# A planned decoder step: sample probabilities spread by one transfer per head pair, second-norm squares summed on VectorE, and other planner figures

## The chip, the cores and the metric

The kernel runs on one core of a Trainium2 chip. The metric is device time in microseconds (us) of one execution, the median of several runs. The engines are called as the profile calls them: PE (TensorE, the matmuls; PEld its weight loads), DVE (VectorE), ACT (ScalarE), POOL (GpSimd), SP (SyncE, which issues all DMAs here). TensorE's clock has two levels, 1.2 and 2.4 GHz; the "granted clock" of a stretch is its share of the higher one.

## What is computed

One inference step of a hybrid decoder layer, for a prompt of 1024 tokens and 8 sample tokens, 1032 columns together, in float32 with d_model 1024:

```python
h = rmsnorm(x, norm1_g)
a, gate, q, k, v, cx, cb, cc, u = split(h @ w_in, 9)     # 256 columns each
ya = silu(layernorm(causal_conv31(a * sigmoid(gate))))
ob = dilated_attention(q, k, v)      # 4 heads of 64; windows (128,1) (512,4) (2048,16)
yc = cb * causal_conv3(cc * cx)
yd = multi_pool(u) @ pool_w * pool_scale
x = x + concat(ya, ob, yc, yd) @ w_out
g, u = split(rmsnorm(x, norm2_g) @ w_gu, 2)
x = x + (silu(g) * u) @ w_down
y = rmsnorm(x, final_g)
# for a sample token: softmax over 3 * 129 cached or own keys per head, then p @ v
```

The outputs are y and the new states: key and value caches, the convolutions' last rows and the pooling's last rows.

## The kernel before, in words

All activations are held transposed, features on the 128 partitions and tokens along the row. The 1032 columns are cut in three chunks of 384, 256 and 392 (c = 0, 1, 2); the last holds the 8 sample tokens. Weights and activations are split into a high and a low part (ACT copies the high part, DVE subtracts), so each product takes three matmuls; the gate, up and down products use a seven-product Strassen scheme on top.

**Stages in time.** Input projection, prompt attention, convolutions and pooling run to about 320 us; the output projection with the second norm from there to about 420; gate and up products to about 850; down products to about 1090; then the last norm.

**What sets the order.** The kernel is written as streams (generators that yield one operation at a time). `Sched.run` picks among them at build time with a cost model of its own: `ready` says when an operation's operands are there, `emit` adds its cost, and the earliest one, with some preference by priority, is emitted next. The result is a fixed order for each engine. On the chip every engine takes its instructions in that order and waits by semaphores.

**DMAs.** `dma` issues on SP's queue. Each transfer uses one of eight semaphores in turn, so that SP waits for the landing of the one eight issues before it. Tiles come from small pools: `rw0/rw1` for raw weights, `t0..t7` for work tiles, `ta0..ta6` for the sample attention, four PSUM banks `mm0, mm1, ac0, ac1` for products.

**The sample attention.** The softmaxed probabilities of 8 samples and 4 heads are a 32x384 tile `s32` (row 4n + head). They are written to DRAM (`psd`). For each sample n and head pair i, `weigh` loads 128x384 gathered values (`vg`), loads two rows of `psd` so that each fills 64 partitions, and DVE multiplies and sums along the row into `o8` (`tensor_tensor_reduce`, an ISA row in the order, line 1329). Sixteen such steps run beside the output projection. The prompt's mixer outputs pass through DRAM as well (`ccT`).

**The second norm.** For each m (8 row blocks of x) and c, `add_x2` adds the projection to x on DVE (`x2[m]`, tiles g7, g9, g10, g15, g14, g16, g11, g0), ACT squares it, and POOL (`ptt`, line 386) adds the squares over m into one tile. `stat2` sums it over partitions with a matmul (`mi`), DVE makes the reciprocal root (`rs_n`), and a matmul (`st`) spreads it. After chunk 2 the first gate products (`raw_pair`, plain float32 at line 398) stand around that sum. x2 is written to DRAM (`x2d`) and read back by `x2_back` in the down stage.

Of the kernel before, what the change touches and what calls it, by code (L numbers as in the profile page):

```python
# [15 lines left out]
MUL, ADD, SUB, MAX = ALU.mult, ALU.add, ALU.subtract, ALU.max  # L16
# [11 lines left out]
DBLK = [[0, 1], [2, 3], [4, 5], [6, 7], [8, 9], [10]]  # L28
# [18 lines left out]


class Op:
    __slots__ = ("eng", "cost", "reads", "writes", "fn", "dep", "size")  # L50

    def __init__(self, eng, cost, reads, writes, fn, size=0):
        self.eng, self.cost, self.fn, self.size = eng, cost, fn, size
        self.reads = [region(a) for a in reads]
        self.writes = [region(a) for a in writes]
        self.dep = None


PLACE = {}
# [15 lines left out]
class Sched:  # L75
# [9 lines left out]
    def __init__(self):  # L85
        self.clock = {"pe": 0.0, "act": 0.0, "dve": 0.0, "pool": 0.0, "sp": 0.0}
        self.hw = self.dma = 0.0
        self.acc = {}
        self.streams = []
        self.log = []  # L90
        self.now = 0.0

    def add(self, prio, name, it):
        self.streams.append([prio, name, it, None])

    def ready(self, op):
        if op.dep is not None:
            return op.dep
        t = 0.0
        eng = op.eng  # L100
        for regs, wr in ((op.reads, False), (op.writes, True)):
            for k, p0, p1, f0, f1 in regs:
                for q0, q1, g0, g1, end, w, e in self.acc.get(k, ()):
                    if (w or wr) and q0 < p1 and p0 < q1 and g0 < f1 and f0 < g1:
                        if e == eng:
                            lat = 0.0 if eng in ("pe", "act") else 0.13
                        else:
                            lat = 0.2 if "pe" in (e, eng) else 0.14
                        t = max(t, end + lat)
        return t  # L110

    def emit(self, st, op):
        s = max(self.clock[op.eng], self.ready(op))
        if op.size:
            self.clock[op.eng] = s + 0.06
            self.hw = max(self.hw, s) + 0.45
            self.dma = max(self.dma, self.hw + 0.65) + op.size / 358e3
            end = self.dma + 0.95
        else:
            cost = op.cost * (2 if op.eng == "pe" and s < self.WARM else 1)  # L120
            self.clock[op.eng] = end = s + cost
        eng = "dma" if op.size else op.eng
        for regs, w in ((op.reads, False), (op.writes, True)):
            for k, p0, p1, f0, f1 in regs:
                l = self.acc.setdefault(k, [])
                if w:
                    l[:] = [x for x in l if not (p0 <= x[0] and x[1] <= p1 and f0 <= x[2] and x[3] <= f1)]
                else:
                    l[:] = [x for x in l if x[5] or x[6] != eng or not (p0 <= x[0] and x[1] <= p1 and f0 <= x[2] and x[3] <= f1)]
                l.append((p0, p1, f0, f1, end, w, eng))  # L130
        r = op.fn()
        self.log.append((op.eng, s, end, st[1], getattr(getattr(r, "ins", None), "name", None)))
# [8 lines left out]
    def run(self):  # L141
        self.waits = {}
        while self.streams:
            moved = True
            while moved:
                moved = False
                for st in list(self.streams):
                    while st[3] is None or (not isinstance(st[3], Op) and st[3]()):
                        try:
                            st[3] = next(st[2])  # L150
                            moved = True
                        except StopIteration:
                            self.streams.remove(st)
                            moved = True
                            break
            if not self.streams:
                break
            best = {}
            for st in self.streams:
                if st[1] == "main":  # L160
                    w = str(self.blocked(st)) if not isinstance(st[3], Op) else "op"
                    if w != getattr(self, "lastw", None):
                        self.lastw, self.t0 = w, self.now
                    elif w != "op":
                        self.waits[round(self.t0, 1)] = (round(self.now - self.t0, 1), w)
                op = st[3]
                if not isinstance(op, Op):
                    continue
                t = max(self.clock[op.eng], self.ready(op))
                best.setdefault(op.eng, []).append((t, st[0], st))  # L170
            if not best:
                raise RuntimeError("stuck: " + ", ".join(f"{x[1]} {self.blocked(x)}" for x in self.streams))
            pick = None
            for eng, l in best.items():
                t0 = min(x[0] for x in l)
                c = min((x for x in l if x[0] <= t0 + self.win(x[1])), key=lambda x: (x[1], x[0]))
                if pick is None or c[0] < pick[0]:
                    pick = c
            st = pick[2]
            op, st[3] = st[3], None  # L180
            self.now = pick[0]
            self.emit(st, op)
# [98 lines left out]
def get(slots, **kw):  # L281
    if not slots.free:
        def cond():
            return bool(slots.free)
        cond.why = slots.tag
        while not slots.free:
            yield cond
    return slots.alloc(**kw)


def wait(cond):
    if not cond():
        yield cond
# [16 lines left out]
def emit(nc, I, O, pools):  # L310
    PLACE.clear()
    S = Sched()
# [14 lines left out]
    def has(*f):  # L327
        return lambda: all(x in flags for x in f)
# [18 lines left out]
    def nfree(a):  # L347
        n = 1
        for _, m in list(a.ap)[1:]:
            n *= m  # L350
        return n
# [33 lines left out]
    def ptt(out, a, b, op):  # L385
        return pool(lambda: GP.tensor_tensor(out, a, b, op), out, (a, b))  # L386
# [4 lines left out]
    def mcost(r):  # L391
        n = nfree(r)
        if r.dtype == F32R:
            return max(0.112, n / 2400 + 0.0133)
        return 2 * max(0.107, n / 1200 + 0.0025)

    def mm(out, l, r, start, stop):
# [2 lines left out]
    def mms(out, items):  # L400

        def go():
            for o, l, r, a, b in items:
                i = PE.matmul(o, l, r, start=a, stop=b, skip_group_check=True)  # L404
            return i
        return Op("pe", sum(mcost(r) for _, _, r, _, _ in items), [x for i in items for x in i[1:3]], (out,), go)

    def trs(out, items):
        def go():
            for o, a, d in items:  # L410
                i = PE.transpose(o, a, d)  # L411
            return i
        return Op("pe", 0.109 * len(items), [x for _, a, d in items for x in (a, d)], (out,), go)

    def dma(out, in_, eng="sp"):
        n = 4
        for _, m in out.ap:
            n *= m
        q = {"sp": nc.sync, "act": nc.scalar, "pool": nc.gpsimd}[eng]
        return Op(eng, 0.06, (in_,), (out,), lambda: q.dma_start(out, in_), size=n)  # L420

    def split(hi, lo, src):
        yield act(hi, src, AF.Copy)
# [219 lines left out]
    for b, js in enumerate(DBLK):  # L643
        for mp in range(4):
            n = len(js) * 512
# [624 lines left out]
    def sample():  # L1270
# [51 lines left out]
        def weigh(n, i):  # L1322
            v = yield from get(TA, shape=[128, 384])
            yield dma(v, I["vg"][n, i])
            b = yield from get(TA, shape=[128, 384])
            for hh in range(2):
                yield dma(b[64 * hh:64 * hh + 64, :], psd[4 * n + 2 * i + hh, :].partition_broadcast(64))
            m = o8[:, i, n:n + 1]
            yield dve(lambda: V.tensor_tensor_reduce(v, v, b, 1.0, 0.0, MUL, ADD, m), v, (v, b), extra=(m,))
            TA.rel(v, b)  # L1330
            todo[0] -= 1
# [43 lines left out]
    def add_x2(m, c, p, sq, fl):  # L1375
        q, n = cols(c), CN[c]
        yield tt(x2[m][:, q], p[:, 0:n], x2[m][:, q], ADD)
        MM.rel(p)
        t = yield from get(TT)
        yield act(t[:, 0:n], x2[m][:, q], AF.Square)  # L1380
        if (sq, c) not in ssq:
            ssq[sq, c] = t
        else:
            s = ssq[sq, c]
            yield ptt(s[:, 0:n], s[:, 0:n], t[:, 0:n], ADD)
            TT.rel(t)
        flags.add(fl + (m, c))

# [153 lines left out]

    def x2_back():
        for m in range(8):
            t = yield from get(G, shape=[128, T])
            yield dma(t, x2d[m])
            x2[m] = t
            flags.add(("x2", m))
# [185 lines left out]

    def calm():

        yield from wait(lambda: S.dma < S.now + 3.5)

    def hload():
        for b, js in enumerate(DBLK):  # L1740
# [416 lines left out]
```

## Time and profile before

| | us |
|---|---|
| median of 3 runs | 1115.37 (1114.7 to 1115.53) |
| profiled execution | 1119.55 |
| its span, first to last instruction | 1117.8 |
| PE busy | 1088.2 (97%) |
| DVE busy | 921.0 (82%) |
| ACT busy | 497.6 (45%) |
| POOL busy | 48.3 (4%) |

The rows that follow come from the profiled execution. Times in them are us from the start of its span. A view of windows gives the busy time of each engine in a stretch; the timeline merges equal instructions and gives, in brackets, the idle time of the engine just before and what ended it; the chain is followed back from the last instruction to what released each step. The DMA view counts packets and lists the transfers by what they write and read.

### The profile page before, as it was taken

To read this page: it belongs to the slowest core of one execution; us is meant where nothing else is said; L and a number is where in the kernel's file an instruction comes from. 1 tells how busy PE (TensorE), PEld (TensorE's weight loads), DVE (VectorE), ACT (ScalarE), POOL (GpSimd) and SP (SyncE) were. 2 spreads that over 40 slices of the span, in tenths; PEclk is the share of its full clock that TensorE was granted. 3 is DMA by queue.
4 is the path that set the end of the run, shared out by engine and by line. 5 is a ranking of instruction groups with operands and counts; after the bars stand their busy time and mean duration, and the time that the engine had idled before them with its cause. 6 is when DMAs were issued, how large, how long until landed. Compare 5 with 4: busy or idle time off the path is not lost.

```text
span 1117.8 us, 21986 instructions
## 1 busy us (share of the span) xinstructions
PE 1088.2 (97%) x8167; PEld 1054.9 (94%) x8167; DVE 921.0 (82%) x2281; ACT 497.6 (45%) x1125; POOL 48.3 (4%) x63
## 2 busy tenths in 40 slices
PE   8999999999998999999999999999999999999995
PEld 5799998999998998999999999999999999999995
DVE  5999999866655498978878777887886999999977
ACT  6564633645533244535444444443543433333332
POOL 0000000000002240000000000000000000000033
PEclk9999999999999998999999999999999999999997
DMA  8042224534388423557457566655638999693103
GB/s 298 1 162 90 102 83 137 198 122 158 117 273 278 153 88 118 178 192 265 170 199 256 172 210 224 209 187 174 204 120 270 388 363 325 229 322 124 38 21 133
DMA packets 104395, 205.39 MB, mean 184 GB/s; under 512 B 11552, under 2 KB 65104, under 8 KB 103760
## 3 DMA queue, kind: packets, MB, share of 16 engines
q1 hardware_dynamic: 104288, 203.99, 53.7%
q8 instruction: 64, 1.05, 0.4%
q14 instruction: 43, 0.35, 0.1%
HBM read 150.98 MB, written 86.87 MB: 213 GB/s over the span
## 4 chain that ended last, share of the span: by engine, by line
PE 70%; DVE 15%; DMA 6%; ACT 2%; issue 2%; SPq 1%; POOL 0%; DVEq 0%; ACTq 0%; POOLq 0%
PE mm L404 37%; PE ac L404 28%; DVE g L369 5%; DVE g L372 2%; DMA t<-kg 2%; PE st L404 2%; DMA ta<-psd 2%; DVE wo L372 1%; DVE t L372 1%; DVE ta L372 1%; DVE h L372 1%; PE st L411 1%; SPq L420 1%; PE mm L398 1%; DMA t<-ccT 1%
## 5 line engine op out<-in xcount | busy, mean ns | idle before, releaser
L404 PE MATMUL mm<-h,wo 128*128 128x256 f32 (+3 forms) x3012 | 475.7, 302 | 3.4 <-ACT wo L362 3.4
L404 PEld LDWEIGHTS mm<-h,wo 128*128 128x128 f32 x3012 | 431.3, 189 | 6.7 <-ACT wo L362 3.5
L404 PE MATMUL ac<-h,wo 128*128 128x256 f32 (+3 forms) x1830 | 273.3, 289 | 0.0
L404 PEld LDWEIGHTS ac<-h,wo 128*128 128x128 f32 x1830 | 248.6, 189 | 0.0
L404 PE MATMUL mm<-g,wo 128*128 128x260 f32 (+1 forms) x879 | 126.4, 282 | 0.0
L404 PEld LDWEIGHTS mm<-g,wo 128*128 128x128 f32 x879 | 114.0, 189 | 0.0
L362 ACT ACTIVATE g<-g 128x260 fp32r<-128x260 f32 (+2 forms) x203 | 75.2, 413 | 83.9 <-DVE g L372 82.2
L372 DVE TENSOR_TENSOR g<-mm,g 128x260 f32<-128x260 f32 (+3 forms) x203 | 85.7, 425 | 27.3 <-PE mm L404 25.2
L404 PE MATMUL ac<-g,wo 128*128 128x260 f32 (+1 forms) x735 | 107.2, 283 | 0.0
L372 DVE TENSOR_TENSOR wo<-rw,wo 128x512 fp32r<-128x512 f32 x140 | 96.2, 690 | 8.8 <-ACT wo L362 8.3
L362 ACT ACTIVATE wo<-rw 128x512 fp32r<-128x512 f32 x140 | 87.1, 625 | 31.1 <-PE mm L404 19.8
L404 PEld LDWEIGHTS ac<-g,wo 128*128 128x128 f32 x735 | 96.2, 189 | 0.0
L372 DVE TENSOR_TENSOR g<-g,g 128x260 f32<-128x260 f32 (+4 forms) x195 | 80.8, 435 | 14.1 <-ACT g L362 7.3
L362 ACT ACTIVATE wo<-t 128x512 fp32r<-128x512 f32 (+1 forms) x103 | 60.8, 590 | 64.0 <-DVE t L372 46.4
L386 POOL TENSOR_TENSOR t<-t,t 128x256 f32<-128x256 f32 (+3 forms) x44 | 43.7, 992 | 886.0 <-ACT t L362 719.3
L369 DVE SCALAR_TENSOR_TENSOR g<-g,parh,g 128x1024 f32<-128x1024 f32 (+2 forms) x90 | 81.6, 923 | 0.4
L372 DVE TENSOR_TENSOR g<-g 128x260 fp32r<-128x260 f32 (+3 forms) x201 | 79.5, 424 | 2.7 <-ACT g L362 2.4
L372 DVE TENSOR_TENSOR g<-ac,g 128x256 f32<-128x256 f32 (+3 forms) x139 | 59.4, 427 | 24.6 <-PE ac L404 20.9
L372 DVE TENSOR_TENSOR wo<-t,wo 128x512 fp32r<-128x512 f32 (+1 forms) x103 | 65.3, 634 | 11.3 <-ACT wo L362 8.8
L362 ACT ACTIVATE t<-g 128x256 f32<-128x256 f32 (+4 forms) x90 | 40.0, 455 | 65.2 <-DVE g L372 47.5
L372 DVE TENSOR_TENSOR g<-t,g 128x260 f32<-128x260 f32 (+4 forms) x151 | 62.3, 431 | 2.5 <-ACT g L362 1.9
L404 PE MATMUL mm<-ta,wo 128*128 128x256 f32 (+1 forms) x357 | 61.6, 281 | 0.4 <-DVE g L372 0.4
(169 smaller groups left out, 1199.4 us busy)
## 6 DMA issues: line engine op xcount, KB each, us to landing
hd<-g SPq DMA_DIRECT2D x74, 260.0 KB, 3.4
hd<-g SPq DMA_DIRECT2D x74, 256.0 KB, 4.2
out_k_old<-cache_k SPq DMA_DIRECT2D x16, 1023.5 KB, 6.1
out_v_old<-cache_v SPq DMA_DIRECT2D x16, 1023.5 KB, 6.8
h<-hd SPq DMA_DIRECT2D x49, 256.0 KB, 6.0
g<-w_gu SPq DMA_DIRECT2D x22, 512.0 KB, 4.2
rw<-w_gu SPq DMA_DIRECT2D x22, 512.0 KB, 4.5
h<-hd SPq DMA_DIRECT2D x40, 260.0 KB, 6.0
```

What stands on the lines that cost most here:

```text
L362: lambda: AE.activation(out, in_, func, **kw))
L369: return dve(lambda: V.scalar_tensor_tensor(out, a, s, b, op0, op1), out, (a, s, b), ptr=aps(s))
L372: return dve(lambda: V.tensor_tensor(out, a, b, op), out, (a, b))
L386: return pool(lambda: GP.tensor_tensor(out, a, b, op), out, (a, b))
L398: return Op("pe", mcost(r), (l, r), (out,), lambda: PE.matmul(out, l, r, start=start, stop=stop, skip_group_check=True))
L404: i = PE.matmul(o, l, r, start=a, stop=b, skip_group_check=True)
L411: i = PE.transpose(o, a, d)
L420: return Op(eng, 0.06, (in_,), (out,), lambda: q.dma_start(out, in_), size=n)
```

## The change

Two operations change. `weigh` spreads its two probability rows with one transfer instead of two. The seven additions of squares of chunk 2 go from POOL to DVE; those of the other chunks stay. The rest changes the planner's figures, and so the order: dearer and later DMAs, 0.4 us of spare time for PE work outside the main stream behind producers other than DMAs, 0.8 us behind DMAs for everything that isn't a DMA, a small surcharge for a wide matmul behind a narrow one, a longer DMA backlog that loads of hidden tiles may meet (`calm`), and `x2_back` waits for block 0's last hidden tile from its fifth tile on. Line numbers after the change are 4 to 6 higher.

```diff
@@ class Sched @@
-    def ready(self, op):
-        if op.dep is not None:
-            return op.dep
+    SPARE, LATE = 0.4, 0.8
+
+    def ready(self, op, spare=0.0, late=0.0):
...
-                            lat = 0.2 if "pe" in (e, eng) else 0.14
+                            lat = (0.2 if "pe" in (e, eng) else 0.14) + (late if e == "dma" else spare)
...
-            self.hw = max(self.hw, s) + 0.45
-            self.dma = max(self.dma, self.hw + 0.65) + op.size / 358e3
-            end = self.dma + 0.95
+            self.hw = max(self.hw, s) + 0.5
+            self.dma = max(self.dma, self.hw + 0.7) + op.size / (300e3 if op.thin else 356e3)
+            end = self.dma + 1.2
...
+            if op.eng == "pe":
+                cost += 0.085 if self.short and not op.thin else 0.0
+                self.short = op.thin
...
-                t = max(self.clock[op.eng], self.ready(op))
+                side = op.eng == "pe" and st[1] != "main"
+                t = max(self.clock[op.eng], self.ready(op, self.SPARE if side else 0.0, 0.0 if op.size else self.LATE))
@@ mcost, trs, dma @@
-            return max(0.112, n / 2400 + 0.0133)
+            return max(0.112, n / 2400 + (0.0133 if n < 300 else 0.0155))
...
-        return Op("pe", 0.109 * len(items), [x for _, a, d in items for x in (a, d)], (out,), go)
+        return Op("pe", 0.112 * len(items), [x for _, a, d in items for x in (a, d)], (out,), go, thin=True)
...
-        return Op(eng, 0.06, (in_,), (out,), lambda: q.dma_start(out, in_), size=n)
+        return Op(eng, 0.06, (in_,), (out,), lambda: q.dma_start(out, in_), size=n, thin=nfree(out) < 512)
@@ weigh @@
-            for hh in range(2):
-                yield dma(b[64 * hh:64 * hh + 64, :], psd[4 * n + 2 * i + hh, :].partition_broadcast(64))
+            yield dma(b[:, :], psd[4 * n + 2 * i:4 * n + 2 * i + 2, :].unsqueeze(1).to_broadcast([2, 64, 384]))
@@ add_x2 @@
-            yield ptt(s[:, 0:n], s[:, 0:n], t[:, 0:n], ADD)
+            yield (ptt if c < 2 else tt)(s[:, 0:n], s[:, 0:n], t[:, 0:n], ADD)
@@ x2_back @@
         for m in range(8):
+            if m > 3:
+                yield from wait(has(("hl", 0, 1, 4, len(DBLK[0]) - 1)))
             t = yield from get(G, shape=[128, T])
@@ calm @@
-        yield from wait(lambda: S.dma < S.now + 3.5)
+        yield from wait(lambda: S.dma < S.now + 5)
```

**SP's queue at the first spreads** (ta tiles are the sample attention's; ccT loads feed the output projection), before:

```order
L420 DMA psd_76<-s32_3151 32x384
L420 DMA ta2_24_3277<-vg 128x384
L420 DMA ta4_25_3278<-vg 128x384
L420 DMA ta6_27_3282<-psd_76 64x384 x2
L420 DMA ta5_26_3280<-psd_76 64x384
L420 DMA t3_197_3300<-ccT_74 128x256
L420 DMA t6_198_3301<-ccT_74 128x256
L420 DMA t0_199_3302<-ccT_74 128x256
```
and after:

```order
L425 DMA psd_76<-s32_3147 32x384
L425 DMA ta2_24_3329<-vg 128x384
L425 DMA ta4_25_3330<-vg 128x384
L425 DMA ta6_26_3332<-psd_76 128x1x384
L425 DMA ta5_27_3334<-psd_76 128x1x384
L425 DMA rw0_19_3379<-w_out 128x1024
L425 DMA ta0_28_3391<-vg 128x384
L425 DMA ta3_29_3393<-psd_76 128x1x384
L425 DMA ta2_30_3399<-vg 128x384
```
The spreads are single 128x1x384 transfers, the ccT loads of chunk 1 have gone ahead of the psd write, and w_out tiles stand between the spreads.

**DVE behind the last products** (ISA rows; g14 is x2 of m=4, h20 the sample chunk's operand, rs_n20 the second norm's chain for chunk 0), before:

```order
L1329 ISA ta3_55_3748,o8_3276<-ta3_55_3748,ta1_56_3750 128x384
L1329 ISA o8_3276 128x1
L372 TENSOR_TENSOR g15_39_3479<-ac1_20_3790,g15_39_3479 128x256
L372 TENSOR_TENSOR pself_3269<-smp_72,pself_3269 128x8
L372 TENSOR_TENSOR g13_27_1163<-pself_3269,o8_3276 128x8
L372 TENSOR_TENSOR pself_3269<-smp_72,pself_3269 128x8
L372 TENSOR_TENSOR g6_35_2706<-pself_3269,o8_3276 128x8
L372 TENSOR_TENSOR h20_3_3483<-g13_27_1163,h20_3_3483 128x392
```
and after:

```order
L1333 ISA ta1_55_3878,o8_3328<-ta1_55_3878,ta0_56_3880 128x384
L1333 ISA o8_3328 128x1
L376 TENSOR_TENSOR pself_3320<-smp_72,pself_3320 128x8
L376 TENSOR_TENSOR g13_27_1207<-pself_3320,o8_3328 128x8
L376 TENSOR_TENSOR pself_3320<-smp_72,pself_3320 128x8
L376 TENSOR_TENSOR g6_35_2752<-pself_3320,o8_3328 128x8
L376 TENSOR_TENSOR h20_3_3463<-g13_27_1207,h20_3_3463 128x392
L376 TENSOR_TENSOR g14_40_3797<-ac1_22_3953,g14_40_3797 128x256
L376 TENSOR_TENSOR h20_3_3463<-g6_35_2752,h20_3_3463 128x392
L381 TENSOR_SCALAR rs_n20_4028<-mi0_14_4024 128x3
L381 TENSOR_SCALAR rs_n20_4028<-rs_n20_4028 128x3
L380 TENSOR_SCALAR rs_n20_4028<-rs_n20_4028 128x3
```
In the new order the chain of chunk 0 stands right behind the last product; before, w_out splits and six x2 adds stood between.

**PE at the broadcast of that chain** (st1_123; ac0_23 is the bank of m=7, chunk 1), after:

```order
L408 MATMUL mm0_59_4037<-h10_2_3243,wo8_49_3713 128x256 x6
L408 MATMUL ac0_23_4082<-h10_2_3243,wo1_52_3822 128x256 x3
L408 MATMUL st1_123_4078<-t6_228_4068,ones_68 128x128 x3
L408 MATMUL ac0_23_4082<-h10_2_3243,wo1_52_3822 128x256 x3
L408 MATMUL ac0_23_4082<-h10_2_3243,wo0_51_3757 128x256 x6
L408 MATMUL ac0_23_4082<-h10_2_3243,wo1_52_3822 128x256 x6
```
and before, where the broadcast st2_123 stands behind all products of its bank:

```order
L404 MATMUL ac0_23_4049<-h10_2_3299,wo9_50_3767 128x256 x6
L404 MATMUL ac0_23_4049<-h10_2_3299,wo8_49_3746 128x256 x6
L404 MATMUL st2_123_4095<-t4_228_4084,ones_68 128x128 x3
L404 MATMUL ac1_24_4093<-h10_2_3299,wo1_52_3814 128x256 x6
L404 MATMUL ac1_24_4093<-h10_2_3299,wo0_51_3791 128x256 x6
L404 MATMUL ac1_24_4093<-h10_2_3299,wo1_52_3814 128x256 x6
```
It has moved 21 matmuls ahead.

## Rows read from the trace of the kernel before

**Rows 1.** The page, busy time of each engine and its share of the span.

```profile
PE 1088.2 (97%) x8167; PEld 1054.9 (94%) x8167; DVE 921.0 (82%) x2281; ACT 497.6 (45%) x1125; POOL 48.3 (4%) x63
```

**Rows 2.** Timeline at two waits of PE: start, us, what, idle time before it.

```profile
347.49 1.81 PE L404 MATMUL mm<-h,wo 128*128 128x384 f32 x7 [3.37 <-ACT wo L362]
...
419.97 1.80 PE L404 MATMUL mi<-ones,t 128*128 128x1 f32 x8 [2.87 <-POOL t L386]
```

**Rows 3.** Windows: PE, PEld, DVE, ACT, POOL busy; PE's granted clock, DMA share, GB/s.

```profile
299.00:360.00 61.00, 57.63 (x362) 57.23 (x362) 31.90 (x86) 21.63 (x49) 5.26 (x6) 0.97 0.80 255
...
417.00:422.00 5.00, 2.13 (x10) 2.03 (x10) 4.93 (x13) 3.45 (x7) 1.10 (x1) 0.81 0.74 255
422.00:428.00 6.00, 6.00 (x18) 4.79 (x18) 4.92 (x19) 1.54 (x3) 0.00 (x0) 0.59 0.00 0
```

**Rows 4.** Instructions that read psd: issue ns min/median/max, first and last start.

```profile
L420 SPq DMA_DIRECT2D ta<-psd x32: 444/487/1904, 302.0 to 351.0; - x32
```

**Rows 5.** Chain that ends last, 299 to 362, one piece: start, us, what.

```profile
318.31 7.79 DMA ta<-psd
```

**Rows 6.** Timeline of DVE around the last products of the sample attention.

```profile
356.75 0.54 DVE L1329 CUSTOM_DVE_ANT_0 ta<-ta,ta 128x384 f32<-128x384 f32 x1
...
371.51 0.16 DVE L377 TENSOR_SCALAR rs_n<-mi 128x3 f32<-128x3 f32 x1 [2.25 <-PE mi L404]
```

**Rows 7.** Timeline of PE at the broadcast of the second norm's first chunk.

```profile
372.12 2.98 PE L404 MATMUL ac<-h,wo 128*128 128x256 f32 x24
375.19 0.94 PE L404 MATMUL st<-t,ones 128*128 128x128 f32 x6
```

**Rows 8.** The page: GB/s in 40 slices, packet counts, the main DMA queue.

```profile
GB/s 298 1 162 90 102 83 137 198 122 158 117 273 278 153 88 118 178 192 265 170 199 256 172 210 224 209 187 174 204 120 270 388 363 325 229 322 124 38 21 133
DMA packets 104395, 205.39 MB, mean 184 GB/s; under 512 B 11552, under 2 KB 65104, under 8 KB 103760
...
q1 hardware_dynamic: 104288, 203.99, 53.7%
```

**Rows 9.** DMA issues: transfers, KB of each, median us from issue to landing where known.

```profile
rw<-w_out SPq DMA_DIRECT2D x12, 512.0 KB, 5.6
...
g<-xR SPq DMA_DIRECT2D x8, 516.0 KB, 5.7
...
ta<-vg SPq DMA_DIRECT2D x16, 192.0 KB, 3.7
...
x2d<-g SPq DMA_DIRECT2D x8, 320.0 KB, 2.8
...
t<-ccT SPq DMA_DIRECT2D x6, 196.0 KB, 6.5
...
out_a_old<-state_a SPq DMA_DIRECT2D x1, 232.0 KB
t<-stp SPq DMA_DIRECT2D x2, 60.0 KB, 3.8
out_p_old<-state_p SPq DMA_DIRECT2D x1, 112.0 KB
prm<-prm SPq DMA_DIRECT2D x1, 50.0 KB, 1.8
...
out_a_tail<-t SPq DMA_DIRECT2D x2, 19.0 KB, 1.5
out_p_tail<-t SPq DMA_DIRECT2D x2, 11.5 KB
t<-stp SPq DMA_DIRECT2D x2, 8.0 KB, 3.2
out_c_tail<-t SPq DMA_DIRECT2D x2, 5.0 KB, 3.2
out_c_old<-state_c SPq DMA_DIRECT2D x1, 8.0 KB
qsd<-tok SPq DMA_DIRECT2D x1, 8.0 KB
```

More of the change, by code (lines that the diff above doesn't have):

```diff
@@ L49, with __init__ @@
 class Op:
-    __slots__ = ("eng", "cost", "reads", "writes", "fn", "dep", "size")
-    def __init__(self, eng, cost, reads, writes, fn, size=0):
-        self.eng, self.cost, self.fn, self.size = eng, cost, fn, size
+    __slots__ = ("eng", "cost", "reads", "writes", "fn", "thin", "size")
+    def __init__(self, eng, cost, reads, writes, fn, size=0, thin=False):
+        self.eng, self.cost, self.fn, self.size, self.thin = eng, cost, fn, size, thin
         self.reads = [region(a) for a in reads]
         self.writes = [region(a) for a in writes]
-        self.dep = None
 PLACE = {}
@@ L91, in __init__ @@
         self.now = 0.0
+        self.short = False
     def add(self, prio, name, it):
         self.streams.append([prio, name, it, None])
-    def ready(self, op):
-        if op.dep is not None:
-            return op.dep
+    SPARE, LATE = 0.4, 0.8
+    def ready(self, op, spare=0.0, late=0.0):
         t = 0.0
@@ L405, in go @@
             return i
-        return Op("pe", sum(mcost(r) for _, _, r, _, _ in items), [x for i in items for x in i[1:3]], (out,), go)
+        return Op("pe", sum(mcost(r) for _, _, r, _, _ in items), [x for i in items for x in i[1:3]], (out,), go,
+                  thin=nfree(items[-1][2]) < 200)
     def trs(out, items):
```

## Prediction

> **What bounds the kernel now.** I read the page's busy times first: TensorE (PE) works 97% of the span and is idle for 1117.8 − 1088.2 = 29.6 us [rows 1], so a change gains only where it takes away a PE wait or a slow stretch, and loses wherever PE is made to wait longer. Second, PE's timeline in the middle of the program: two waits stand out [rows 2]. At 347.49 PE had waited 3.37 us for a w_out half that ScalarE (ACT) and VectorE (DVE) split late, because both stood in line behind a load of ccT. At 419.97 it had waited 2.87 us for the last sum of the second norm's squares, which GpSimd (POOL) adds. The windows behind the second wait [rows 3] show what follows it: from 422 to 428 PE is busy throughout at a granted clock of 0.59, so it spent that stretch mostly at the lower of its two levels (1.2 and 2.4 GHz), while 417 to 422 has 0.81. Third, the sample attention's probability spreads (`ta<-psd`), which the change rewrites: 32 of them are issued from 302.0 to 351.0 [rows 4], and one of them, issued at 318.31, lies on the chain that ends last for 7.79 us [rows 5]. They are close to critical already: SP's queue and DVE go through them in order.
>
> **The spread, one transfer per head pair.** Before, each of 16 (sample, pair) steps issues two 64x384 transfers whose source is one row read 64 times, so the outermost size on both sides is 64. After, it is one 128x384 transfer whose source is two rows, each read 64 times: the outermost size is 2 at the source and 128 at the destination. What the outermost size does can be read from the count of small packets. The SP queue's program holds 636 transfers. If each closes with 16 small marks that is 10,176; transfers with rows under 512 B are the `stp` loads of 60 and 8 KB, the `prm` load of 50 KB and the three kinds of tails [rows 9], 11 transfers of 128 rows, 1,408 packets; together 11,584. The page has 11,552 [rows 8], 32 fewer. Exactly four transfers have an outermost size of eight, the three state copies and `tok` [rows 9]; with eight marks instead of 16 for each the count comes out exactly. So a transfer is shared among as many DMA engines as its outermost size allows, up to 16, and I take it that two source rows leave two engines. No row shows a two-engine transfer.
>
> The Trainium skill says it outright (DMA: Bandwidth & Descriptors, section Why a DMA increments its semaphore by 16 and not by 1): the hardware queue takes the largest number of engines up to 16 that divides the slowest dimension of both patterns. The eight-row transfers of this trace agree. The same page's rules for kernel authors speak for the change: two transfers to disjoint partition halves should be one of 128 partitions; the sum by that rule alone is the first rival's.
>
> Price of one: 192 KB is 196.6 kB, 98.3 kB on each of two engines. What an engine moves: over the whole run 203.99 MB in 53.7% of 16 x 1117.8 us, 21.2 kB/us; in the stretch itself 255 GB/s at a share of 0.80, 255/(16 x 0.80) = 19.9 [rows 3, 8]; in the fullest slice of the page 388/16 = 24.3. I take 23, nearer the fullest slice, since these two engines never run out of work. One spread holds them for 98.3/23 = 4.27 us, sixteen for 68.4 us (64.7 at 24.3, 79.0 at 19.9), where before the same bytes cost all engines 4.3 us each in total.
>
> The two engines also carry their sixteenth of everything else that SP issues between the first and the last spread: in the new order 14 `vg` loads, 7 w_out tiles, 8 xR tiles, 6 to 7 ccT pieces of 196 KB and 4 x2d stores of 320 KB. By the sizes in [rows 9] that is 14x192 + 7x512 + 8x516 + 7x196 + 4x320 = 13,052 KB, 13.4 MB, 0.835 MB for each engine: 36.3 us (34.4 to 42.0). A transfer is complete only with its slowest engine, and SP keeps few transfers in flight, so all of these fall to the pace of the two. Sum: 68.4 + 36.3 = 104.7 us (99.1 to 121).
>
> **Where that reaches PE.** The psd write stands where it stood, as the softmax ahead of it does, so the first spread starts near 302.0 [rows 4]; with about 2 us until bytes land, the sixteenth is complete at 302 + 2 + 104.7 = 408.7. In the new DVE order the last two products (`weigh`) stand ahead of the x2 add of m=4, the two adds into h20 and the whole rstd chain of the second norm's first chunk; and PE has the broadcast of that chain (`st1_123`) three matmuls into `ac0_23`. PE runs ahead by its four banks and then waits there. From the last product to the broadcast: product 0.54 [rows 6], seven short adds near 2 (an estimate by 0.54 for the wide ones), chain 375.19 − 371.51 = 3.7 [rows 6, 7]: 6.2 us, so the broadcast runs at 414.9. Before it ran at 375.19 behind all 24 products of its bank; now 21 of them come after it, 21 x 2.98/24 = 2.6 us [rows 7], so its like place was 372.6. **Shift: 414.9 − 372.6 = +42.3 us** (36 at 24.3 kB/us, 59 at 19.9). The wait at 347.49 is inside this shift; its removal gives nothing of its own. While PE waits again and again, its clock may be low as after 419.97, and the out-projection's products in between would take longer: 0 to 8 us more, an estimate from the six slow microseconds there [rows 3].
>
> **The squares on DVE.** Seven 128x392 adds move from POOL to DVE. Before, POOL's last add made PE wait 2.87 us, and the slow clock behind it cost about 3 more (6.00 busy us at 0.59 and 2.13 at 0.81, 6 x 0.41 + 2.13 x 0.19 = 2.9) [rows 2, 3]. On DVE such an add is about as long as a product of that width, 0.54 [rows 6]; the last one stands two short rows behind the last x2 add, and PE asks for the sum one matmul earlier than before. I take −6 us (bounds −3 and −7). DVE is full there (4.93 of 5 us [rows 3]), so some of it comes back as waits for the Strassen sums: +1.5 (0 to 4). **x2 loads** behind block 0's last h load: 8 loads, first needed some ten us later, +0.3 (0 to 1.5).
>
> **The planner's figures.** The spare time that the planner now leaves ahead of side work on PE can remove small waits before 299. Of the 29.6 us of idle time the two named waits are 6.2; the rest is spread over many places, the start and the tail among them. I take −3 (0 to −6); it comes ahead of the spreads, so it moves the whole stretch. Behind the last wait PE starts at a low clock: +2.5 (0 to 4, by the 6 us at 0.59). Pieces of the order that only change places cost nothing: PE's matmuls are the same but for three warm-up ones.
>
> Sum: 42.3 − 6 + 1.5 + 0.3 − 3 + 2.5 = **+37.6 us**. The profiled execution took 1119.55 us (span 1117.8), 4.2 above the median 1115.37; 1119.55 + 37.6 = 1157.1, and against the median **1153**.
>
> **Rivals.** (1) *The spread keeps 16 engines* (the small source row is laid out over the 128 destination rows). Then the queue has 16 transfers fewer at about 0.49 us of issue each [rows 4], the ccT load behind 347.49 is issued earlier and I give it 2.5 of the 3.37; with −6 − 3 + 1.8 the sum is −9.7: **1106**. For it: a 128-row destination. Against it: the count of the eight-row transfers. It decides if the first spread lands within 4 us. (2) *Two engines, but hidden*: out-projection work and four banks cover more, or different transfers use different engines, so that each spread costs latency and not throughput. One spread of 4.3 us instead of two of 96 KB then adds 1 or 2 us to a chain that now and then waits for it: −9.7 + 2.5 (the wait at 347.49 stays) + 2 to 10: **1110 to 1120**. Against it: sixteen in about 50 us at 4.27 leave those engines 68 us of work in 50, which no order hides. (3) *Worse than forecast*: engines at 19.9 kB/us and PE at the lower clock all through: 1153 + 16 + 8 = **1177**.
>
> **How the numbers follow.** Forecast with its own range 1140 to 1170 and rival 3 together 0.87; rival 1 0.09; rival 2 0.04. About 0.2% (2.2 us) is what a measurement of this kernel can tell from no change. Faster 0.10, same 0.02, slower 0.88. The range holds the forecast, rival 3 and some play below: 1130 to 1182, with rivals 1 and most of 2 left out.
>
> **What would show it.** In the DMA view `ta<-psd` is 16 of 192 KB, from issue to landing 7 us or more at the median; the packets under 512 B fall by 16 x 16 for the absent transfers and by 16 x 14 for the marks of those left, 480 in all. DVE's idle time for `ta<-psd` comes to 50 us or more between 305 and 410, PE's busy share there falls near a half, and the gate products begin about 38 us later. Wrong it is if those loads land in under 5 us, or if PE keeps over 90% from 300 to 400. Apart from that, no wait of PE on a POOL add near the second norm should be left.

## The result, and the profile after

The changed kernel takes 1158.93 us (1158.62 to 1159.7), the kernel before 1115.45 in the runs beside it: a ratio of 1.0397, 95% interval 1.0376 to 1.0419, so 43.5 us slower. The prediction was 1153, with 1130 to 1182 around it.

PE's share falls, its busy time hardly changes. The page of the changed kernel, its busy times and its packets, beside [rows 1] and [rows 8]:

```profile
PE 1096.9 (95%) x8173; PEld 1061.4 (92%) x8173; DVE 922.2 (80%) x2288; ACT 497.7 (43%) x1125; POOL 34.2 (3%) x56
...
DMA packets 103916, 205.39 MB, mean 177 GB/s; under 512 B 11073, under 2 KB 64625, under 8 KB 103281
```

PE is idle for 61.0 us of its span instead of 29.6. The packets under 512 B are 479 fewer than in [rows 8]; 480 were expected if 32 transfers that close with 16 marks each (small packets that signal a landing) become 16 that close with two. SP's own queue, which carries the spreads, has exactly 480 fewer than the 104288 of [rows 8]:

```profile
q1 hardware_dynamic: 103808, 203.99, 52.1%
```

The windows say where the time went. Columns as in [rows 3]; all of it lies between 300 and 450, and DMA is no busier there on average than the 0.80 of [rows 3]. Before:

```profile
300.00:350.00 50.00, 46.63 (x300) 46.30 (x299) 24.53 (x66) 16.69 (x37) 3.04 (x3) 0.98 0.79 244
350.00:400.00 50.00, 49.91 (x317) 49.71 (x317) 30.28 (x83) 16.38 (x35) 15.00 (x14) 0.98 0.53 193
400.00:450.00 50.00, 46.26 (x218) 41.45 (x218) 45.46 (x117) 24.70 (x62) 8.55 (x5) 0.93 0.28 98
```

and after:

```profile
250.00:300.00 50.00, 49.99 (x365) 47.51 (x364) 38.48 (x107) 25.99 (x54) 0.00 (x0) 1.00 0.41 132
300.00:350.00 50.00, 45.81 (x293) 45.04 (x292) 19.41 (x49) 16.29 (x37) 1.01 (x1) 0.97 0.56 171
350.00:400.00 50.00, 25.93 (x131) 24.27 (x130) 13.79 (x34) 8.06 (x17) 5.23 (x6) 0.81 0.52 171
400.00:450.00 50.00, 38.94 (x240) 38.73 (x239) 26.94 (x82) 14.24 (x33) 6.15 (x8) 0.85 0.31 110
450.00:500.00 50.00, 49.13 (x275) 45.02 (x274) 49.16 (x134) 26.17 (x67) 0.00 (x0) 1.00 0.29 103
```

An average over 16 engines can hide two that are full, and the experiments below speak for two: from 350 to 400 the DMA share is 0.52 while PE stands still for 24 of the 50 us. The spreads themselves, and who waits for them (issue ns min/median/max, first and last start; then us and times):

```profile
L425 SPq DMA_DIRECT2D ta<-psd x16: 492/499/1332, 308.9 to 402.2; - x16
...
  DVE ta L1333: 57.6, 14
```

Sixteen issues stretch over 93 us, where 32 took 49 [rows 4]. The chain that ends last in this stretch (start, us, what) runs through them, and through other transfers that stand behind them in SP's queue:

```profile
309.59 10.46 DMA ta<-psd
...
322.46 9.71 DMA rw<-w_out
...
332.55 11.58 DMA t<-ccT
344.20 7.91 DMA ccT<-t
352.18 9.88 DMA t<-ccT
...
364.42 10.18 DMA ta<-psd
...
388.77 12.88 DMA g<-xR
401.75 0.41 DVE g L376
402.16 12.09 DMA ta<-psd
414.33 0.09 issue
414.41 0.56 DVE ta L1333
```

A w_out tile, a ccT piece and an xR tile take 9 to 13 us from issue to landing, with medians of 5.6, 6.5 and 5.7 in [rows 9], although none of them changed. The last spread lands at 414.3, 105.4 us after the first was issued. PE's timeline shows the waits (start, us, what, idle time before it):

```profile
363.69 6.23 PE L408 MATMUL ac<-h,wo 128*128 128x384 f32 x24 [9.01 <-DVE g L376]
372.53 8.57 PE L408 MATMUL mm<-h,wo 128*128 128x384 f32 x48 [2.60 <-DVE g L376]
384.65 6.14 PE L408 MATMUL ac<-h,wo 128*128 128x384 f32 x24 [3.56 <-ACT wo L366]
398.57 4.55 PE L408 MATMUL ac<-h,wo 128*128 128x256 f32 x24 [7.77 <-DVE g L376]
405.09 0.73 PE L408 MATMUL mi<-ones,t 128*128 128x1 f32 x6
420.94 1.65 PE L408 MATMUL st<-t,ones 128*128 128x128 f32 x6 [11.06 <-DVE t L380]
...
464.05 1.00 PE L408 MATMUL mi<-ones,t 128*128 128x1 f32 x8
469.31 1.05 PE L408 MATMUL st<-t,ones 128*128 128x128 f32 x8
```

PE names DVE and ACT, never a DMA. What these two wait for stands one step back: on DVE mostly the spreads, on ACT also a ccT piece and a w_out tile that land late:

```profile
362.08 0.53 ACT L366 ACTIVATE h<-t 128x392 fp32r<-128x392 f32 x1 [8.95 <-DMA t<-ccT]
...
383.45 1.15 ACT L366 ACTIVATE wo<-rw 128x512 fp32r<-128x512 f32 x2 [8.35 <-DMA rw<-w_out]
```

The longest wait is the one before the first broadcast, 11.06 us until 420.94, the place that the prediction named. In part of the work between the waits the granted clock is low too: 24 products of 128x384 take 6.23 us at 0.68 (363.7 to 369.9), while 48 take 8.57 at 1.00 (372.5 to 381.1).

### The profile page after: what moved, and what is told of

It reads as the page before. It is cut to its first block, busy times and chain, and to the rows that moved or that the text cites. A ratio compares the mean times of both kernels' runs of the same rounds, so it can differ in the third digit from the quotient of the medians.

```text
span 1157.9 us, 21952 instructions
## 1 busy us (share of the span) xinstructions
PE 1096.9 (95%) x8173; PEld 1061.4 (92%) x8173; DVE 922.2 (80%) x2288; ACT 497.7 (43%) x1125; POOL 34.2 (3%) x56
## 4 chain that ended last, share of the span: by engine, by line
PE 72%; DVE 15%; DMA 8%; issue 2%; ACT 2%; SPq 1%; DVEq 0%; ACTq 0%
PE mm L408 36%; PE ac L408 29%; DVE g L373 6%; DMA ta<-psd 3%; PE ac L402 2%; PE st L408 2%; DMA t<-ccT 2%; PE st L402 1%; DVE g L376 1%; SPq L425 1%; DMA g<-xR 1%; PE mm L402 1%; DVE ta L376 1%; DVE wo L376 1%; DVE h L376 1%
## 5 line engine op out<-in xcount | busy, mean ns | idle before, releaser
L408 PE MATMUL mm<-h,wo 128*128 128x256 f32 (+3 forms) x3018 | 487.4, 302 | 3.9 <-DVE g L376 2.6
L408 PE MATMUL ac<-h,wo 128*128 128x256 f32 (+3 forms) x1812 | 287.3, 294 | 25.7 <-DVE g L376 22.1
L408 PEld LDWEIGHTS ac<-h,wo 128*128 128x128 f32 x1812 | 256.3, 194 | 27.5 <-DVE g L376 13.9
L366 ACT ACTIVATE g<-g 128x260 fp32r<-128x260 f32 (+3 forms) x202 | 74.8, 412 | 73.0 <-DVE g L376 70.4
L376 DVE TENSOR_TENSOR g<-g 128x256 fp32r<-128x256 f32 (+3 forms) x220 | 86.8, 424 | 5.6 <-ACT g L366 5.0
L373 DVE SCALAR_TENSOR_TENSOR g<-g,parh,g 128x384 f32<-128x384 f32 (+2 forms) x90 | 81.3, 924 | 0.4
L376 DVE TENSOR_TENSOR g<-g,g 128x256 f32<-128x256 f32 (+4 forms) x176 | 73.5, 439 | 8.5 <-ACT g L366 4.4
L366 ACT ACTIVATE g<-ac 128x256 f32<-128x256 f32 (+1 forms) x88 | 33.6, 382 | 72.3 <-PE ac L408 68.6
L376 DVE TENSOR_TENSOR g<-t,g 128x256 f32<-128x256 f32 (+4 forms) x150 | 62.1, 435 | 2.1 <-ACT g L366 1.3
```

Source lines behind the costliest of these rows:

```text
L366: lambda: AE.activation(out, in_, func, **kw))
L373: return dve(lambda: V.scalar_tensor_tensor(out, a, s, b, op0, op1), out, (a, s, b), ptr=aps(s))
L376: return dve(lambda: V.tensor_tensor(out, a, b, op), out, (a, b))
```

## Experiments

**One size alone: the outermost size of the spread's source.** Four kernels use the changed planner's figures and the squares on DVE, but two 64x384 transfers per head pair again. They have the same order on every engine and move the same bytes; only the source pattern of the spread differs, K x (64/K) repeats of one row:

```diff
-            yield dma(b[:, :], psd[4 * n + 2 * i:4 * n + 2 * i + 2, :].unsqueeze(1).to_broadcast([2, 64, 384]))
+            for hh in range(2):
+                yield dma(b[64 * hh:64 * hh + 64, :], psd[4 * n + 2 * i + hh:4 * n + 2 * i + hh + 1, :].unsqueeze(0).to_broadcast([2, 32, 384]))
```

This is K = 2; for 4 and 8 the sizes are `[4, 16, 384]` and `[8, 8, 384]`. For 64 the line is the one of the kernel before (`partition_broadcast(64)`).

> The changed kernel, but each pair is spread by two 64x384 transfers again, whose source has an outermost size of 64 (each 96 KB over 16 engines). Theory (two engines hold each spread of the change): the 68 us that the spreads kept two engines shrink to 8.5 on each of 16, the wait at the second norm's first broadcast goes, and what is left is the squares on VectorE and the planner's figures: 1104 to 1110 us. Rival (the planner's new order makes the loss): about 1155 us as with the change. Rival (one large landing instead of two is the cost): 1104 to 1110 as well; the three runs beside this one tell it from the theory.

> The same with 8 times 8 repeats: outermost size 8. Theory: 24.6 kB on each of eight engines for every pair, 17 us in all beside 36 of the other transfers, 53 us, close to the 49 us over which the kernel before issued its spreads: nearly hidden, 1105 to 1114 us, at most 6 above the run with the outermost size of 64. Rival (any size under 16 is slow alike): 1150 to 1165.

> The same with 4 times 16 repeats: outermost size 4, two transfers per pair, the same order on every engine. Theory: 49.2 kB on each of four engines for every pair, 34 us in all beside 36 of the other transfers, 70 us from the first spread to the last instead of 105: 34 us less than with the outermost size of 2, so 1120 to 1130 us. Rival (one large landing): 1104 to 1110. Rival (any size under 16 is slow alike, for another reason): 1150 to 1165.

> As the run with two 64x384 transfers per pair and with the same order on every engine, but the source row is written as 2 times 32 repeats, so that the outermost size is 2. Theory (as many engines as the outermost size allows): two engines again hold 98.3 kB for every pair, 4.2 to 4.3 us, 67 to 69 us in all: 1150 to 1165 us. Rival (one large landing instead of two small ones is the cost): 1104 to 1110, as two transfers of 96 KB are there. Rival (reading one row of memory 64 times over is slow, whatever the engines): the same time as with the outermost size of 64.

| outermost size | us | before beside it | ratio to before (95%) | spreads issued, first to last | broadcast at |
|---|---|---|---|---|---|
| 64 | 1111.63 | 1112.57 | 0.9989 (0.9968 to 1.0009) | 309.9 to 361.3 | 376.61 |
| 8 | 1118.03 | 1112.57 | 1.0035 (1.0019 to 1.0051) | 309.8 to 365.2 | 379.40 |
| 4 | 1127.32 | 1112.57 | 1.0115 (1.0081 to 1.0149) | 308.9 to 375.0 | 389.92 |
| 2 | 1160.55 | 1112.57 | 1.0421 (1.0381 to 1.0460) | 309.1 to 405.0 | 422.12 |

The time follows the outermost size with nothing else changed. Two of the four miss their expected range: 1111.63 lies above 1104 to 1110 (the planner's figures gained nothing, see below), and 1118.03 above 1105 to 1114. The packet rows of the runs with 64, 8, 4 and 2 count the marks:

```profile
DMA packets 104395, 205.39 MB, mean 185 GB/s; under 512 B 11552, under 2 KB 65104, under 8 KB 103760
```

```profile
DMA packets 104139, 205.39 MB, mean 184 GB/s; under 512 B 11296, under 2 KB 64848, under 8 KB 103504
```

```profile
DMA packets 104011, 205.39 MB, mean 182 GB/s; under 512 B 11168, under 2 KB 64720, under 8 KB 103376
```

```profile
DMA packets 103947, 205.39 MB, mean 177 GB/s; under 512 B 11104, under 2 KB 64656, under 8 KB 103312
```

From 11,552 they fall by 256, 384 and 448, which is 32 transfers times 8, 12 and 14: each closes with 16, 8, 4 and 2 marks. From 4 to 2 the broadcast moves by 32.2 us (389.92 to 422.12), 34 were expected: 16 pairs put 786 kB more on each of two engines, and 786 kB in 32.2 us is 24.4 kB/us, an estimate of what an engine moves that never rests, beside 24.3 in the fullest slice of [rows 8]. Had the transfers taken turns on different engines, no engine would have had more to move, so they seem to use the same two each time. From 8 to 4 the broadcast moves by 10.5 and not by 17, probably because at 8 the engines' work is nearly hidden already; at 8 the whole costs 6.4 us more than at 64 (1118.03 to 1111.63; 5.1 by the ratios), about the 6 that were expected at most. The run with two transfers and outermost size 2 is as slow as the change with one (ratio 1.0421 and 1.0397), so one large landing is not the cause; and one row is read 64 times over in all four, so that isn't either. Only the source's size was varied, and only by powers of two; the destination keeps its 64 or 128 rows.

**One transfer on 16 engines.** The psd store writes each row eight times, and the spread reads 16 rows eight times each:

```diff
-    psd = dr.tile([32, 384], F32, name="psd")
+    psd = dr.tile([32, 8, 384], F32, name="psd")
...
-        yield dma(psd[:, :], s32[0:32, 0:384])
+        yield dma(psd[:, :, :], s32[0:32, 0:384].unsqueeze(1).to_broadcast([32, 8, 384]))
...
-            yield dma(b[:, :], psd[4 * n + 2 * i:4 * n + 2 * i + 2, :].unsqueeze(1).to_broadcast([2, 64, 384]))
+            yield dma(b[:, :], psd[4 * n + 2 * i:4 * n + 2 * i + 2].rearrange("r c f -> (r c) f").unsqueeze(1).to_broadcast([16, 8, 384]))
```

> The changed kernel with its one 128x384 transfer per head pair, but each row of probabilities is written eight times into memory (one store of 32 x 8 x 384, 384 KB instead of 48), so that the spread's source is 16 rows read eight times each: outermost size 16. Theory (engines by the outermost size): all 16 engines serve each spread and the loss goes though the number of transfers is that of the change: 1108 to 1116 us, near the run with two transfers of outermost size 64 (1111.63), up to 2 us more for the larger store on the chain. Rival (one large landing per pair is the cost): 1150 to 1165.

Measured 1109.67 beside 1114.29, ratio 0.9953 (0.9938 to 0.9968). The single transfer is as it is in the change; with 16 source rows the loss is gone. The packets under 512 B are 11,296, 256 fewer than with two transfers of size 64: 16 transfers fewer, and 16 marks for each of those left. The broadcast shows part of why it even beats those two transfers (ratio 0.9989): there PE waits and runs at a granted clock of 0.80 behind the wait (376.6 to 385), here it hardly waits and has 1.00 (374.3 to 382). PE's timeline of the two, outermost size 64 first:

```profile
376.61 1.40 PE L408 MATMUL st<-t,ones 128*128 128x128 f32 x6 [2.89 <-DVE t L380]
```

```profile
374.32 0.94 PE L408 MATMUL st<-t,ones 128*128 128x128 f32 x6 [0.22 <-DVE t L380]
```

**The spread alone, in the order of before.** The kernel before with the change's line in `weigh` and nothing else:

> The kernel before with its own planner figures and its squares on GpSimd, with only the spread changed to one transfer per head pair (outermost size 2). Theory: the two engines need some 105 us for the stretch in any order, so about the whole loss of the change comes with this edit alone: 1145 to 1170 us. Rival (the loss needs the new planner's order, which sets the first norm chain behind the last product): under 1130.

Measured 1158.25 beside 1114.29, ratio 1.0394 (1.0365 to 1.0422): the whole loss, without the planner's figures and with the squares on POOL. DVE waits for the spreads as in the change; this run's rows of psd:

```profile
L420 SPq DMA_DIRECT2D ta<-psd x16: 498/504/607, 301.5 to 385.1; - x16
...
  DVE ta L1328: 57.4, 15
```

57.4 us there, 57.6 in the change. Against two transfers of size 64 in the same order, the single spread costs about 44 us in the order of before (1 to 1.0394) and 45 in the changed one (0.9989 to 1.0397). In this run PE's longest wait is 12.87 us, until 344.84, and the first broadcast at 414.66 has none. So the order around the first broadcast, on which the prediction's shift was worked out, decides where PE waits and hardly how much it loses.

**The squares.** In the order of before:

```diff
-            yield ptt(s[:, 0:n], s[:, 0:n], t[:, 0:n], ADD)
+            yield (ptt if c < 2 else tt)(s[:, 0:n], s[:, 0:n], t[:, 0:n], ADD)
```

> The kernel before with only the last columns' seven square sums moved from GpSimd to VectorE. Theory (the two engines hold each other up there, and the wait for the last sum brings a slow clock): the wait of 2.9 us and about 3 us of slow clock go, 3 to 7 us less than before. Rival (VectorE is full there, what it takes on comes back as waits for its own sums): within 2 us of before.

Measured 1109.46 beside 1114.29, ratio 0.9949 (0.993 to 0.9969): 5.7 us gained by the ratio, 4.8 by the medians. The wait for the last sum is gone, and with it the slow clock. First the sum's matmul on PE and one of the DVE adds ahead of it, then the window:

```profile
413.80 0.95 PE L404 MATMUL mi<-ones,t 128*128 128x1 f32 x8
```

```profile
412.76 0.57 DVE L372 TENSOR_TENSOR t<-t,t 128x392 f32<-128x392 f32 x1
```

```profile
400.00:450.00 50.00, 49.49 (x280) 45.62 (x279) 49.41 (x135) 26.31 (x69) 0.00 (x0) 1.00 0.29 106
```

The sum starts without a wait at 413.80 instead of 419.97 after 2.87 us [rows 2]. Of these 6.2 us, 2.7 are there at the first broadcast already (372.49 instead of 375.19), where both orders are still the same: the two profiled executions differ by that much. From the sum to its own broadcast it takes 4.78 us (418.58) instead of 8.66. The granted clock of the window is 1.00 where before had 0.93, with 0.59 from 422 to 428 [rows 3], and DVE is busy for 49.41 of 50 us: full, but PE doesn't wait for it by more than it did.

**The planner's figures.** The run with outermost size 64, its squares back on POOL, so that only the planner's figures differ from before:

> The run with two transfers of outermost size 64 (1111.63 beside 1112.57), with the seven square sums back on GpSimd: the planner's new figures alone. Theory (the squares on VectorE gain some 5 us and the planner's figures lose them again elsewhere): 3 to 7 us above that run, so 1114 to 1119. Rival (neither does anything): within 2 us of it.

Measured 1116.70 beside 1114.29, ratio 1.0019 (1.0001 to 1.0036): they gain nothing and may cost 2 us. Two more pairs differ in the figures alone: 0.9989 against 0.9949 (two transfers of size 64, squares on DVE) and 0.9953 against 0.9936 (16 source rows, squares on DVE; the second is the last run below). There the figures cost 4.5 and 2 us, with some 3 and 2 us of noise in either difference. All three point the same way: a cost of a few us. Against 0.9989 with the squares on DVE, 1.0019 says that the squares gain 3.3 us in this order, give or take 3. The waits of PE in this run (line, what ended the wait, us in total, times, longest):

```profile
PE st L408 <- DVE t L380: 3.4, 3, 2.9
PE mi L408 <- POOL t L390: 3.3, 2, 3.0
```

The 3.37 us for the w_out half at 347.49 [rows 2] are not among them. But the length of that wait varies: in the run with the squares alone, whose order up to there is that of before, it is 1.39 us (until 346.31). And in the new order the softmax ends later, so that the psd write goes out at 305.9 instead of 299.9. What else the figures cost was not found.

**The two operations without the figures, on 16 engines.** The kernel before with the 16-row spread, alone and with the squares on DVE:

> The kernel before, its planner figures and its GpSimd sums kept, with one spread per head pair from rows stored eight times (outermost size 16). Theory (on 16 engines one transfer instead of two saves issue time on SP, so the ccT load behind PE's wait at 347.49 goes out earlier): 1 to 4 us less than before. Rival (what the same spread gained in the changed kernel belongs to that order, where the second norm's first chain stands right behind the last product): within 1.5 us of before.

> The same with the last columns' seven square sums on VectorE as well: the change's two operations without its planner figures, and with the spread on 16 engines. Theory (the gains add up: 0.9949 for the sums alone, and 1 to 4 us for the spread): 0.991 to 0.994 of before. Rival (the spread adds nothing in this order): 0.994 to 0.997.

Measured 1114.01 beside 1114.23, ratio 1.0002 (0.9987 to 1.0018), and 1107.89, ratio 0.9936 (0.992 to 0.9952). In the order of before the single spread gains nothing, so the expected 1 to 4 us did not come, although PE's wait at 347.49 is absent from this run's profile; what it gained over two transfers in the changed order (0.9953 against 0.9989) belongs to that order. The second kernel, just inside its expected range, is the fastest of all, 6.3 us under before and about 51 under the change, though its lead over the squares alone (0.9949) lies within both intervals. So the change's aim can be had: 16 source rows instead of two.

## Why the prediction was right, step by step

**The two engines.** The step that carried the forecast was read from a packet count: four transfers with eight rows closed with eight marks. The runs with 64, 8, 4 and 2 show the same for marks and time. The Trainium skill states this (DMA: Bandwidth & Descriptors, section Why a DMA increments its semaphore by 16 and not by 1), and its rules for kernel authors, row Use all 16 engines, warn of an outermost size under 16; the four runs agree with both. The row Two transfers to disjoint partition halves, of the same table of the Trainium skill, favours one 128-partition transfer; here that cost 4% with two source rows (1.0394) and nothing with 16 (1.0002), both in the order of before. One figure beside the price is wrong, though no sum uses it: before, the spreads' bytes cost each of 16 engines 196.6 kB, at 23 kB/us 8.5 us, not 4.3; and the lower bound of the shift, 36, comes out as 36.7.

**The length of the stretch.** 104.7 us of engine work and 2 for the start were forecast from first issue to last landing; measured are 105.4 (308.9 to 414.3). The rate of 23 kB/us was a choice between 19.9 and 24.3; the step from outermost size 4 to 2 gives 24.4, so the engines were probably somewhat faster, and some 5 us of the stretch were not theirs.

**The start.** The prediction let the psd write stand at its old 299.9, "as the softmax ahead of it does". The softmax did not. Its last step on DVE, before:

```profile
299.38 0.41 DVE L376 TENSOR_SCALAR s<-s,sm 32x385 f32<-32x385 f32 x1
```

and after:

```profile
304.86 0.41 DVE L380 TENSOR_SCALAR s<-s,sm 32x385 f32<-32x385 f32 x1
```

It runs 5.5 us later, and the write went out at 306.0, 6.1 us later. The ccT loads that now stand ahead of the write on SP, the last of them issued by 305.95, can account only for the 0.6 us between. The delay comes with the new order: the run with the figures alone has the write at 305.9. These 6 us make up about the whole miss in the time of the broadcast.

**From the last landing to the broadcast.** 6.2 us forecast, 6.6 measured (414.3 to 420.94). So the broadcast came at 420.94 instead of 414.9, against its like place 372.6 a shift of 48.3 and not 42.3: by and large the late start. The path to this broadcast is the right one for the changed order, but the loss does not need it, as the spread alone in the order of before shows.

**The squares.** −6 forecast, with bounds −3 and −7: −5.7 in the order of before (0.9949), −3.3, give or take 3, in the changed one. In the changed kernel the sum (`mi`, 464.05) comes 43.1 us behind the first broadcast, before 419.97 − 372.6 = 47.4, and from the sum to its own broadcast it takes 5.26 us (469.31) where the slow clock had made it 8.66. Before's row for that broadcast:

```profile
428.63 1.05 PE L404 MATMUL st<-t,ones 128*128 128x128 f32 x8
```

Of the small terms, +1.5 for the Strassen sums and +0.3 for the x2 loads hardly show: PE's wait at those sums is 0.87 us before and after, and in the down stage it idles for 0.1 us (740 to 1040) where before it did not idle (700 to 1000). The +2.5 for the low clock behind the last wait does: 0.74 from 421 to 430 is 9 x 0.26 = 2.3 us.

**The planner's figures.** Wrong: −3 was put on them, the three pairs of runs show +2 to +4.5. The spare time was given to PE's side work on the ground that 29.6 us of idle time were spread over many places; it was not worked out for any of them. From 250 to 300 PE does gain (49.99 busy us, before 48.62), from 100 to 150 it loses as much (48.62 where before had 50.00).

**The sum.** Per span: +48.3 at the broadcast and −8.2 behind it make +40.1 (1157.9 − 1117.8), where +42.3 − 1.7 − 3 = +37.6 was forecast. So the forecast came 9.0 short at the broadcast (6.0 for the start, 3 for the figures) and was 6.5 too high behind it. That these nearly cancel is luck; what carried the prediction is the two engines and the length of their stretch. The median moved by 43.5, since the profiled execution of before lay 4.2 above its median and that of the change 0.8.

**The signs.** The packets fell as stated, DVE's idle time for the spreads is 57.6 us where 50 or more was stated, and no wait of PE on a POOL add is left near the second norm. PE is busy for 71.7% of 300 to 400, under the 90% that would have refuted the forecast; but near a half it comes only from 350 to 400, and it is 73% from 305 to 410. The plain gate products begin 47.5 us later (461.46, before 413.92), not 38. The DMA view gives no landing time for the spreads of the change; those on the chain above take 10 to 12 us.

## What to carry to other kernels

Before merging small transfers look at the outermost size of both patterns as they are written, source and destination. Here a source size of 2, 4 or 8 left each spread with that many marks and, by the times, that many DMA engines, though its destination had 64 or 128 rows; other transfers in the queue landed late with it, while the mean DMA share looked half empty. The count of small packets on the page of the kernel before told it ahead of the change. If one transfer is to spread a few rows over partitions, store them several times: with 16 rows to read, the loss was gone. Two transfers of outermost size 64 were as good in the order of before (1.0002). And an addition on POOL that PE waits for can cost nearly as much again in slow clock behind the wait: from the sum of the squares to its broadcast PE took 8.66 us in the kernel before and 7.00 in the run with only the 16-row spread, but 4.78 in both runs of that order with the sums on DVE.

## What the runs showed of the hardware that was not expected

With an outermost size of 8 the engines' work of 17 us is small, and yet the run is 6.4 us above that with 64; its spreads take 587 ns to issue at the median instead of 479, and PE's wait at the first broadcast is 4.41 us instead of 2.89. How much of the 6.4 is issue and how much is landing was not told apart. And PE loses twice: in the changed kernel from 350 to 400 it is busy for 25.93 us at a granted clock of 0.81, so that part of what it does between its waits runs at the lower level; that the waits hide this until the last of them is argued, not shown. After the last one 421 to 430 still has 0.74.
